# Scores of two heads on 64 rows each, 64-column state products in runs, and the state half's norm two chunks later, in a hybrid S5 and attention encoder layer

## The chip, the cores and the metric

One core of one Trainium2 chip runs the whole layer. The metric is the device time of one execution in microseconds (us). The engines are PE (TensorE, the matrix products), DVE (VectorE), ACT (ScalarE), POOL (GpSimd) and SP (SyncE, which issues most transfers).

## What is computed

One encoder layer on a sequence of 256 frames of width 2048, all in float32. Attention heads and a state space model (S5) share the input projection; their outputs are normed, joined, projected and added to the input; a convolved feed-forward part follows. Cut to what matters here:

```python
proj = x @ w_in                                  # q | k | v | u, 1024 columns each
scores = einsum(q, k) * 64 ** -0.5 + bias        # 16 heads of 64, chunk-causal band
attn = softmax(scores) @ v
s = scan(exp(dt * a), u @ B);  ssm = Re(C s) + D * u     # 64 groups, 64 states, 16 channels
ssm = gelu(ssm);  ssm = ssm * sigmoid(ssm @ w_glu + b_glu)
x = LayerNorm(alpha * x + concat(rmsnorm(attn), rmsnorm(ssm)) @ w_out)
hidden = gelu(causal_dwconv3(x @ W_gate)) * (x @ W_val)
out = LayerNorm(alpha * x + hidden @ w_ffn_out)
```

## The kernel before

**Main products.** Every weight matrix is streamed in chunks of 128x1024 floats. The loop `run` takes them in a fixed order; for chunk j it issues the load of chunk j+7 on SP (L148), and has chunk j+3 split into a high part `hi` (ACT, L163) and the rest `lo` (DVE, L164). Four buffers hold each of `raw`, `hi` and `lo`, so a split waits until PE has used the chunk four before. A chunk of the k and q projections (`kq`, chunks 32 to 63, four to each pair of heads: two of k, two of q) is 16 products on PE (L209 with 512 columns, L211 with 256), one of the v projection (chunks 24 to 31 near this change) is 12 (L245, L247, L249). These are called mains below.

**Side products.** The state space model and the attention of each pair of heads run as generators beside that loop. Small products go into a queue through `put(f, cost)`. After each main, `fill()` adds one credit (at most two are kept) and issues queued products until their costs have used it up, so a cost of 0.25 lets four products through for one main, and a cost of 0 lets all through at once. A scheduler then orders each engine's instructions by its own model, so the order on an engine is not that of the code alone.

**The parts that the change touches.** `ll` (L778) gives the local states: 4 groups x 2 parts (real, imaginary), named ll00 to ll31, each of 16 products that fill 64 of the 128 columns of the array (`tile_position=(0, 64 * g2)`), at cost 0.25; `drained()` makes a generator wait until the queue is empty. `ks` (L873) gives the kernel of the first block in 64 products at cost 0.5. When all `ll` are done (`loc_done`), POOL clears the tile `Kt` (L900), which takes the place of `loc`, SP fills it by eight small transfers (L907), and DVE runs the scan over chunks of the sequence (L844 to L847, 21 steps of four instructions). `CM` (L943, L944, L948) are the output matrices of the state space model, computed on DVE, the last of them `CM3`. `y` (L973) multiplies `Kt`, `X` and `CM`. For each pair of heads j, `evac_k` adds the two halves of the k product into `kz[0]` and `kz[1]` (L501, 64 partitions each; the other 64 partitions of each were cleared at the start), `evac_q` writes `qt` (L506), `scores(h)` gives S of head h in two products over all 128 rows (L1048, L1049), DVE adds the bias and finds the maximum (L1061), ACT takes the exponential, PE transposes (T, L1071) and multiplies by v (O, L1084). `kz` and `qt` have one buffer each, so the next pair's are written after this pair's S.

**The norm of the state half.** `evac_os(0)` first calls `rms(1)`: two products with a column of ones on PE (L1028) over `sqs`, to which POOL adds a square for each of eight blocks (L1012), a root on ACT, a reciprocal on DVE; then DVE scales and adds (L1168) and takes statistics (L1174). It stands after chunk (nb, c) = (1, 0) of the output projection of the state half (`os`). The chunks of that stage are 12 mains each; chunks of later column blocks are split into tiles that are kept (`held`).

Of the kernel before, what the change touches and what calls it, by code (L numbers as in the profile page):

```python
# [118 lines left out]
class Builder:  # L119
# [15 lines left out]
    def put(self, f, cost=1.0):  # L135
        self.queue.append((f, cost))
# [155 lines left out]
    def plan_phase1(self):  # L292
# [117 lines left out]
        for nb in range(4):  # L410
            for c in range(4):
# [26 lines left out]
                if nb == 0:  # L438
                    post = None
                elif (nb, c) == (1, 0):  # L440
                    post = lambda: self.evac_os(0, cur["po", 0], (0, 1))
                elif c < 3:
                    post = None
                self.add(I["wo"][8 * nb + 4 + c], mm, post, hold)

        self.kz = [ap.tile([P, SEQ], F32, name=f"kz{h}") for h in range(2)]
        self.qt = ap.tile([P, SEQ], F32, name="qt")
# [48 lines left out]
    def evac_k(self, j, ps):  # L496
        nc = self.nc
        t = self.evac_ab(ps, f"kb{j}")
        for h in range(2):
            r = slice(64 * h, 64 * h + 64)  # L500
            nc.vector.tensor_tensor(self.kz[h][r], ps[r, 0:SEQ], t[r], op=ALU.add)  # L501

# [6 lines left out]
    def s5_load(self):  # L509
# [9 lines left out]
        nc.gpsimd.memset(loc[64:128, :, :, :, 0:64], 0.0)  # L519
        nc.gpsimd.memset(self.kz[0][64:128], 0.0)  # L520
        nc.gpsimd.memset(self.kz[1][0:64], 0.0)

# [229 lines left out]
    def s5_loc(self):  # L752
# [20 lines left out]
        def ll(q, ri):  # L773
# [11 lines left out]
            for i in range(8):  # L785
                for g2 in range(2):
                    put(lambda i=i, g2=g2: mm(i, g2), 0.25)
            put(evac, 0)

        def both(f, pg):  # L790
            for ri in range(2):
                f(pg, ri)
# [26 lines left out]
        yield  # L819
        both(ll, 2)  # L820
        both(ll, 3)
        yield from drained()
# [39 lines left out]
    def s5_kstack(self):  # L862
# [14 lines left out]
        for i in range(16):  # L877
            for ri in range(2):
                for h in range(2):
                    self.put(lambda i=i, ri=ri, h=h: mm(i, ri, h), 0.5)  # L880
        while self.queue:
# [154 lines left out]
    def attention(self, j):  # L1036
        nc, ap, I = self.nc, self.ap_, self.I
        kz, qt = self.kz, self.qt
        v = self.res1
# [5 lines left out]

        def scores(h):
            ps = st["S", h] = self.bank(5 + h, f"S{j}{h}")
            nc.tensor.matmul(ps[:, 0:256], lhsT=qt[:, P:2 * P], rhs=kz[h], start=True, stop=True)  # L1048
            nc.tensor.matmul(ps[:, 256:384], lhsT=qt[:, 0:P], rhs=kz[h][:, 0:P], start=True, stop=True)  # L1049

# [62 lines left out]
        load(1)  # L1113
        scores(0)
        scores(1)
        yield
# [272 lines left out]
```

## Time and profile before

| what | value |
|---|---|
| median of 3 runs | 1141.27 us (1140.03 to 1142.17) |
| the profiled execution's own time | 1141.15 us |
| span of its profile | 1139.3 us |
| PE busy | 1110.3 us, 97% |
| DVE busy | 774.4 us, 68% |
| ACT busy | 566.6 us, 50% |
| mean granted clock of PE | 0.991 |

Times in rows count from the start of the span. An instruction's row gives its start, its duration, engine, line and operation, the tiles (out<-in), sizes, a count, and in brackets how long the engine stood idle before it and what ended that. A float32 product shows as two rows on PE (x2), and durations of neighbours overlap, so the cost of a product on PE is read from start to start. A granted clock of 1.00 is 2.4 GHz, 0.50 is 1.2 GHz.

### The profile page before, as it was taken

The numbers are of one execution on the slowest core, as the hardware profiler recorded it, in microseconds if no ns is written. First come the engines' busy times: TensorE is split into PE (matmuls) and PEld (weight loads), VectorE is DVE, ScalarE is ACT, GpSimd is POOL, SyncE is SP. The second block draws the span as 40 slices with busy tenths as digits, with TensorE's granted clock in tenths as the row PEclk, the third lists the DMA queues.
The fourth block names the chain that finished last, engine by engine and source line by source line (L and its number), as shares of the span: only waits on it lengthen the run. The fifth ranks groups of instructions, "written<-read, shape, count | busy, mean of one in ns | idle before, by whom it ended". The sixth has DMA issues, their size and how long they took to land.

```text
span 1139.3 us, 17905 instructions
## 1 busy us (share of the span) xinstructions
PE 1110.3 (97%) x6980; PEld 948.8 (83%) x6980; DVE 774.4 (68%) x1230; ACT 566.6 (50%) x882; POOL 75.5 (7%) x75
## 2 busy tenths in 40 slices
PE   8999979999999999999999999999999999999996
PEld 6887768888887888888888888888888888888885
DVE  7996889946588776666666666666666575454555
ACT  5455325537575565555555555555555443433350
POOL 2021300000011000000000000000000550000002
PEclk9999979999999999999999999999999999999998
DMA  8886334534766366666666666666666876666661
GB/s 303 279 226 164 118 122 139 162 96 138 244 188 201 108 204 186 185 188 185 188 188 188 186 187 186 186 185 185 189 186 187 307 223 197 190 198 190 192 195 74
DMA packets 61572, 212.03 MB, mean 186 GB/s; under 512 B 7344, under 2 KB 10800, under 8 KB 60592
## 3 DMA queue, kind: packets, MB, share of 16 engines
q1 hardware_dynamic: 59728, 204.18, 58.9%
q0 software_dynamic: 1472, 6.29, 1.8%
q8 instruction: 54, 0.88, 0.3%
q10 hardware_dynamic: 288, 0.43, 0.1%
q14 instruction: 30, 0.25, 0.1%
HBM read 207.46 MB, written 3.41 MB: 185 GB/s over the span
## 4 chain that ended last, share of the span: by engine, by line
PE 93%; DVE 4%; ACT 1%; issue 1%; DMA 1%; SPq 0%; POOL 0%; ACTq 0%; POOLq 0%
PE f L231 29%; PE f L224 15%; PE d L245 7%; PE d L249 7%; PE d L247 7%; PE kq L209 5%; PE u L209 2%; PE kq L211 2%; PE oa L249 1%; PE oa L245 1%; PE oa L247 1%; PE u L211 1%; PE glu L209 1%; DVE lo L164 1%; PE os L249 1%; PE os L245 1%
## 5 line engine op out<-in xcount | busy, mean ns | idle before, releaser
L164 DVE TENSOR_TENSOR lo<-raw,hi 128x1024 fp32r<-128x1024 f32 (+1 forms) x358 | 446.3, 1249 | 210.6 <-ACT hi L163 207.0
L163 ACT CAST hi<-raw 128x1024 fp32r<-128x1024 f32 (+1 forms) x358 | 374.3, 1047 | 300.0 <-PE d L249 116.9
L231 PE MATMUL f<-x1s,hi 128*128 128x512 f32 (+1 forms) x1408 | 487.2, 396 | 1.5 <-DVE x1s L1211 1.5
L224 PE MATMUL f<-x1s,lo 128*128 128x256 f32 x1408 | 380.0, 281 | 0.0
L231 PEld LDWEIGHTS f<-x1s,hi 128*128 128x128 f32 x1408 | 258.8, 188 | 57.6 <-DVE x1s L1211 1.8
L224 PEld LDWEIGHTS f<-x1s,lo 128*128 128x128 f32 x1408 | 265.8, 189 | 8.6
L247 PE MATMUL d<-lo,hid 128*128 128x512 f32 (+1 forms) x360 | 133.4, 371 | 0.0
L245 PE MATMUL d<-hi,hid 128*128 128x512 f32 (+1 forms) x360 | 133.4, 370 | 0.0
L249 PE MATMUL d<-hi,hid 128*128 128x512 f32 (+1 forms) x360 | 133.3, 370 | 0.0
L209 PE MATMUL kq<-xs,hi 128*128 128x512 f32 x240 | 92.8, 422 | 5.1 <-DVE qt L506 2.6
L247 PEld LDWEIGHTS d<-lo,hid 128*128 128x128 f32 x360 | 67.9, 188 | 11.7
L249 PEld LDWEIGHTS d<-hi,hid 128*128 128x128 f32 x360 | 67.8, 188 | 11.7
L245 PEld LDWEIGHTS d<-hi,hid 128*128 128x128 f32 x360 | 67.9, 188 | 11.5
L211 PE MATMUL kq<-xs,lo 128*128 128x256 f32 x240 | 69.8, 291 | 0.0
L209 PEld LDWEIGHTS kq<-xs,hi 128*128 128x128 f32 x240 | 47.0, 196 | 15.8 <-DVE qt L506 2.7
L1319 ACT COPY ga<-f 128x256 f32<-128x256 f32 x44 | 16.4, 372 | 83.3 <-PE f L231 83.3
L1326 DVE TENSOR_TENSOR gp<-f,ga 128x256 f32<-128x256 f32 x44 | 18.8, 426 | 45.6 <-ACT ga L1319 45.6
L1319 ACT COPY va<-f 128x256 f32<-128x256 f32 x44 | 16.4, 372 | 66.1 <-PE f L231 66.1
L1338 DVE TENSOR_TENSOR va<-f,va 128x256 f32<-128x256 f32 x44 | 18.7, 425 | 43.0 <-ACT va L1319 43.0
L211 PEld LDWEIGHTS kq<-xs,lo 128*128 128x128 f32 x240 | 47.2, 197 | 0.8
L209 PE MATMUL u<-xs,hi 128*128 128x512 f32 x120 | 43.5, 401 | 0.0
L1305 POOL DMA_DIRECT2D gb<-rows x4 | 2.2, 554 | 531.6 <-PE f L231 531.6
(228 smaller groups left out, 1366.9 us busy)
## 6 DMA issues: line engine op xcount, KB each, us to landing
raw<-wf SPq DMA_DIRECT2D x176, 512.0 KB, 3.7
raw<-wd SPq DMA_DIRECT2D x88, 512.0 KB, 4.1
raw<-wkq SPq DMA_DIRECT2D x32, 512.0 KB, 3.7
raw<-wo SPq DMA_DIRECT2D x32, 512.0 KB, 4.0
raw<-wu SPq DMA_DIRECT2D x16, 512.0 KB, 4.7
raw<-wv SPq DMA_DIRECT2D x15, 512.0 KB, 6.2
raw<-wg SPq DMA_DIRECT2D x8, 512.0 KB, 3.7
gb<-rows POOLq DMA_DIRECT2D x4, 1024.0 KB, 13.1
```

The source lines that it names most:

```text
L163: self.nc.scalar.copy(hi[:, c], raw[:, c])
L164: self.nc.vector.tensor_tensor(lo[:, c], raw[:, c], hi[:, c].bitcast(F32), op=ALU.subtract)
L209: nc.tensor.matmul(ps, start=first and kk == 0, stop=False, **h)
L211: nc.tensor.matmul(ps[:, 0:SEQ], start=False, stop=False, **l)
L224: nc.tensor.matmul(th(ps), lhsT=lo[:, w], rhs=th(x), start=False, stop=False)
L231: nc.tensor.matmul(ps[:, c], lhsT=hi[:, w], rhs=x[:, c], start=start and part is None, stop=stop)
L245: nc.tensor.matmul(ps, lhsT=ah, rhs=wh, start=first and kk == 0, stop=False)
L247: nc.tensor.matmul(ps, lhsT=ah, rhs=wl, start=False, stop=False)
L249: nc.tensor.matmul(ps, lhsT=al, rhs=wh, start=False, stop=last and kk == 1)
L1319: self.nc.scalar.copy(tv, v[:, :, 1])
L1326: nc.vector.tensor_tensor(g[:, 2:].rearrange("p (t c) -> p t c", t=2), p0, t, op=ALU.add)
L1338: nc.vector.tensor_tensor(tv, p0, tv, op=ALU.add)
```

## The change

The two adds of `evac_k` become one add into one tile `kt` of 128 partitions; the memsets of `kz` go. `scores` issues four products for both heads, each over 64 rows of the array (rows 0 to 63 for head 0, 64 to 127 for head 1), 256 columns for both heads first, then 128 for both. The cost of the `ll` and `ks` products becomes 0, and a `drained()` stands between ll2 and ll3. `evac_os(0)` moves from after chunk (1, 0) to after chunk (1, 2).

```diff
--- before.py
+++ after.py
@@ -437,13 +437,13 @@
                     hold = lambda m=4 * nb + c - 8: self.hold1(m)
                 if nb == 0:
                     post = None
-                elif (nb, c) == (1, 0):
+                elif (nb, c) == (1, 2):
                     post = lambda: self.evac_os(0, cur["po", 0], (0, 1))
                 elif c < 3:
                     post = None
                 self.add(I["wo"][8 * nb + 4 + c], mm, post, hold)
 
-        self.kz = [ap.tile([P, SEQ], F32, name=f"kz{h}") for h in range(2)]
+        self.kt = ap.tile([P, SEQ], F32, name="kt")
         self.qt = ap.tile([P, SEQ], F32, name="qt")
         self.sqs = ap.tile([P, SEQ], F32, name="sqs")
         self.cm_ready = self.mb_ready = 0
@@ -496,9 +496,7 @@
     def evac_k(self, j, ps):
         nc = self.nc
         t = self.evac_ab(ps, f"kb{j}")
-        for h in range(2):
-            r = slice(64 * h, 64 * h + 64)
-            nc.vector.tensor_tensor(self.kz[h][r], ps[r, 0:SEQ], t[r], op=ALU.add)
+        nc.vector.tensor_tensor(self.kt, ps[:, 0:SEQ], t, op=ALU.add)
 
     def evac_q(self, j, ps):
         nc = self.nc
@@ -517,8 +515,6 @@
         loc = self.loc = bp.tile([P, 2, 2, 8, P], F32, tag="d1", name="loc")
         nc.gpsimd.memset(loc[0:64, :, :, :, 64:128], 0.0)
         nc.gpsimd.memset(loc[64:128, :, :, :, 0:64], 0.0)
-        nc.gpsimd.memset(self.kz[0][64:128], 0.0)
-        nc.gpsimd.memset(self.kz[1][0:64], 0.0)
 
     def s5_late_load(self):
         nc, I = self.nc, self.I
@@ -784,7 +780,7 @@
                 nc.scalar.copy(self.L8[:, ri, q * 8:q * 8 + 8], v[:, :, 56:64])
             for i in range(8):
                 for g2 in range(2):
-                    put(lambda i=i, g2=g2: mm(i, g2), 0.25)
+                    put(lambda i=i, g2=g2: mm(i, g2), 0)
             put(evac, 0)
 
         def both(f, pg):
@@ -818,6 +814,7 @@
             yield
         yield
         both(ll, 2)
+        yield from drained()
         both(ll, 3)
         yield from drained()
         self.loc_done = True
@@ -877,7 +874,7 @@
         for i in range(16):
             for ri in range(2):
                 for h in range(2):
-                    self.put(lambda i=i, ri=ri, h=h: mm(i, ri, h), 0.5)
+                    self.put(lambda i=i, ri=ri, h=h: mm(i, ri, h), 0)
         while self.queue:
             yield
         ps = st[0]
@@ -1035,7 +1032,7 @@
 
     def attention(self, j):
         nc, ap, I = self.nc, self.ap_, self.I
-        kz, qt = self.kz, self.qt
+        kt, qt = self.kt, self.qt
         v = self.res1
         st = {}
 
@@ -1043,10 +1040,15 @@
             b = st["b", h] = ap.tile([P, 256], F32, tag="band", bufs=2, name=f"bd{j}{h}")
             nc.sync.dma_start(b, I["band"][2 * j + h])
 
-        def scores(h):
-            ps = st["S", h] = self.bank(5 + h, f"S{j}{h}")
-            nc.tensor.matmul(ps[:, 0:256], lhsT=qt[:, P:2 * P], rhs=kz[h], start=True, stop=True)
-            nc.tensor.matmul(ps[:, 256:384], lhsT=qt[:, 0:P], rhs=kz[h][:, 0:P], start=True, stop=True)
+        def scores():
+
+            for h in range(2):
+                st["S", h] = self.bank(5 + h, f"S{j}{h}")
+            for t in range(2):
+                for h in range(2):
+                    r = slice(64 * h, 64 * h + 64)
+                    o, q, n = ((st["S", h][:, 0:256], slice(P, 2 * P), 256), (st["S", h][:, 256:384], slice(0, P), 128))[t]
+                    nc.tensor.matmul(o, lhsT=qt[r, q], rhs=kt[r, 0:n], start=True, stop=True, tile_position=(64 * h, 0))
 
         def soft(h):
 
@@ -1111,8 +1113,7 @@
 
         load(0)
         load(1)
-        scores(0)
-        scores(1)
+        scores()
         yield
         soft(0)
         yield
```

The cost 0 also changes what the scheduler puts where. On PE, before, ll1 was interleaved with the mains of chunk 30 (`v12` and `v15` are v's sums, `hi30` and `lo30` the chunk's parts):

```order
L245 MATMUL v12_920<-hi30_1066,xs_78 128x512
L778 MATMUL ll10_1203<-up_638,loc_90 64x64 x5
L247 MATMUL v12_920<-lo30_1067,xs_78 128x512
L778 MATMUL ll10_1203<-up_638,loc_90 64x64 x4
L249 MATMUL v12_920<-hi30_1066,xs_78 128x512
L778 MATMUL ll10_1203<-up_638,loc_90 64x64 x4
L245 MATMUL v15_921<-hi30_1066,xs_78 128x512
L778 MATMUL ll10_1203<-up_638,loc_90 64x64 x3
L778 MATMUL ll11_1225<-up_638,loc_90 64x64
L247 MATMUL v15_921<-lo30_1067,xs_78 128x512
```

Now it is in one run after the first main of chunk 27 (`lt` are transposes that prepare ll):

```order
L247 MATMUL v15_918<-lo26_869,xs_78 128x512
L249 MATMUL v15_918<-hi26_868,xs_78 128x512
L245 MATMUL v12_917<-hi27_911,xs_78 128x512
L774 MATMUL ll10_1132<-up_635,loc_89 64x64 x16
L774 MATMUL ll11_1151<-up_635,loc_89 64x64 x16
L758 MATMUL lt30_1170<-ident_69,MB_176 128x128 x2
L247 MATMUL v12_917<-lo27_912,xs_78 128x512
```

All 32 products of ll1 moved together and three chunks earlier. ll2, which was in groups of about four between mains too, now has 21 products in a run and 11 single ones, each between two mains of chunk 36; ll3 is one run of 32 after chunk 37.

On PE at the first pair's scores, before (chunks 36 and 37 of k of the second pair):

```order
L209 MATMUL kq10_1492<-xs_78,hi36_1316 128x512
L211 MATMUL kq10_1492<-xs_78,lo36_1317 128x256
L1048 MATMUL S00_1532<-kz0_83,qt_85 128x256
L1049 MATMUL S00_1532<-kz0_83,qt_85 128x128
L1048 MATMUL S01_1535<-kz1_84,qt_85 128x256
L1049 MATMUL S01_1535<-kz1_84,qt_85 128x128
L209 MATMUL kq10_1492<-xs_78,hi37_1346 128x512
L211 MATMUL kq10_1492<-xs_78,lo37_1347 128x256
```

and now (chunk 35 is the last of q of the first pair, chunk 38 the first of q of the second; chunks 36 and 37 are done by then):

```order
L206 MATMUL kq02_1436<-xs_78,lo35_1333 128x256
L207 MATMUL kq02_1436<-xs_78,hi35_1332 128x512
L970 MATMUL y0_2367<-up_635,Kt_1424 32x64 x4
L970 MATMUL y1_2506<-up_635,Kt_1424 32x64
L1051 MATMUL S00_1532<-kt_83,qt_84 128x256
L1051 MATMUL S01_1533<-kt_83,qt_84 128x256
L1051 MATMUL S00_1532<-kt_83,qt_84 128x128
L1051 MATMUL S01_1533<-kt_83,qt_84 128x128
L209 MATMUL kq12_1580<-xs_78,hi38_1468 128x512
```

The scores stand directly behind the last chunk of their own q, and the first five products of `y` on `Kt` stand ahead of them; before, those products stood later, behind the scores, T and the first O.

On DVE, from the split of chunk 38 to `qt` of the first pair, before:

```order
L164 TENSOR_TENSOR lo38_1452<-raw38_1265,hi38_1451 128x1024
L844 TENSOR_TENSOR kcm_87<-X_869,QI_181 128x512
L845 TENSOR_TENSOR kcm_87<-X_869,kcm_87 128x512
L846 TENSOR_TENSOR kcm_87<-kcm_87,X_869 128x512
L506 SCALAR_TENSOR_TENSOR qt_85<-kq02_1352,qb0_1473 128x256
L847 TENSOR_TENSOR X_869<-kcm_87 128x64x8
```

where two more pieces of four such rows for CM3 (L943, L944, L948) stood between later steps of the scan. Now:

```order
L941 TENSOR_TENSOR kcm_86<-prm_79 128x512
L945 TENSOR_TENSOR CM3_1461<-kcm_86 64x32x16 x2
L940 TENSOR_TENSOR kcm_86<-prm_79 128x512
L941 TENSOR_TENSOR kcm_86<-prm_79 128x512
L945 TENSOR_TENSOR CM3_1461<-kcm_86 64x32x16 x2
L164 TENSOR_TENSOR lo40_1539<-raw40_1403,hi40_1538 128x1024
L841 TENSOR_TENSOR kcm_86<-X_866,QI_178 128x512
L842 TENSOR_TENSOR kcm_86<-X_866,kcm_86 128x512
L843 TENSOR_TENSOR kcm_86<-kcm_86,X_866 128x512
L164 TENSOR_TENSOR lo41_1575<-raw41_1434,hi41_1574 128x1024
L844 TENSOR_TENSOR X_866<-kcm_86 128x64x8
L504 SCALAR_TENSOR_TENSOR qt_84<-kq02_1436,qb0_1490 128x256
```

All of CM3 stands ahead of the scan's first step, and `qt` has the splits of chunks 40 and 41 and a whole step of the scan (L841 to L844 now) ahead of it. At the norm of the state half, 19 mains that stood behind the two products of `rms` now stand ahead of them, and on DVE three splits stand ahead of its reciprocal.

## Rows read from the trace of the kernel before

**Rows 1.** What PE waited for, over the whole span: the waiting line, the releaser, us in total, times, the longest.

```profile
PE kq L209 <- DVE qt L506: 2.6, 1, 2.6
PE kq L209 <- DVE kz L501: 2.5, 2, 2.1
PE T L1071 <- ACT sT L1065: 2.4, 2, 2.0
```

**Rows 2.** Stretches of the span: from:to, its length, then busy us (and instructions) of PE, PEld, DVE, ACT and POOL, the granted clock of PE, the share and rate of the DMA engines. The first rows are whole stages, the last four are 2 us each.

```profile
131.00:145.00 14.00, 14.00 (x82) 12.25 (x81) 13.52 (x26) 5.68 (x11) 3.39 (x1) 1.00 0.60 168
145.00:177.00 32.00, 23.61 (x125) 19.27 (x124) 27.50 (x61) 11.32 (x31) 0.00 (x0) 0.79 0.36 112
177.00:222.00 45.00, 45.00 (x280) 40.11 (x279) 44.32 (x106) 25.89 (x67) 0.00 (x0) 1.00 0.52 157
...
400.00:1139.00 739.00, 728.45 (x3949) 627.52 (x3947) 458.41 (x561) 352.27 (x483) 38.00 (x24) 1.00 0.63 191
...
150.00:152.00 2.00, 0.00 (x0) 0.00 (x0) 2.00 (x5) 0.00 (x0) 0.00 (x0) 0.55 0.48 74
...
156.00:158.00 2.00, 2.00 (x10) 1.68 (x10) 2.00 (x7) 0.00 (x0) 0.00 (x0) 0.74 0.00 0
...
162.00:164.00 2.00, 0.55 (x3) 0.31 (x3) 1.88 (x3) 1.31 (x6) 0.00 (x0) 0.96 0.52 209
...
170.00:172.00 2.00, 2.00 (x11) 1.73 (x10) 0.32 (x1) 1.05 (x1) 0.00 (x0) 0.83 0.00 0
```

**Rows 3.** Mains of kq on PE: the first after a long wait and two more at half clock, the first after another long wait, then two that stand three pairs of mains apart at full clock.

```profile
152.36 0.80 PE L209 MATMUL kq<-xs,hi 128*128 128x512 f32 x1 [2.58 <-DVE qt L506]
...
153.17 0.63 PE L209 MATMUL kq<-xs,hi 128*128 128x512 f32 x1
...
153.81 0.63 PE L209 MATMUL kq<-xs,hi 128*128 128x512 f32 x1
...
165.66 0.79 PE L209 MATMUL kq<-xs,hi 128*128 128x512 f32 x1 [2.09 <-DVE kz L501]
...
176.91 0.40 PE L209 MATMUL kq<-xs,hi 128*128 128x512 f32 x1
...
177.97 0.40 PE L209 MATMUL kq<-xs,hi 128*128 128x512 f32 x1
```

**Rows 4.** ll on PE: the run of ll0 between two mains of v, then two mains 42 apart with nothing between them, then a group of four ll products (eight rows) between two mains.

```profile
84.47 0.48 PE L249 MATMUL v<-hi,xs 128*128 128x512 f32 x1
84.88 2.08 PE L778 MATMUL ll<-up,loc 128*64 128x64 f32 x64
...
86.98 0.48 PE L245 MATMUL v<-hi,xs 128*128 128x512 f32 x1
...
87.76 0.39 PE L245 MATMUL v<-hi,xs 128*128 128x512 f32 x1
...
97.29 0.39 PE L245 MATMUL v<-hi,xs 128*128 128x512 f32 x1
...
98.92 0.50 PE L249 MATMUL v<-hi,xs 128*128 128x512 f32 x1
99.35 0.45 PE L778 MATMUL ll<-up,loc 128*64 128x64 f32 x8
99.73 0.50 PE L245 MATMUL v<-hi,xs 128*128 128x512 f32 x1
```

**Rows 5.** The scores of one head (its two lines, two rows each) and the first main behind both heads' scores, on PE.

```profile
142.03 0.59 PE L1048 MATMUL S<-kz,qt 128*128 128x256 f32 x2
...
142.46 0.38 PE L1049 MATMUL S<-kz,qt 128*128 128x128 f32 x2
...
143.25 0.47 PE L209 MATMUL kq<-xs,hi 128*128 128x512 f32 x1
```

**Rows 6.** DVE from the last ll to the first scores, and the two adds into kz of a later pair.

```profile
130.75 1.23 DVE L164 TENSOR_TENSOR lo<-raw,hi 128x1024 fp32r<-128x1024 f32 x1 [3.49 <-ACT hi L163]
131.89 0.69 DVE L844 TENSOR_TENSOR kcm<-X,QI 128x512 f32<-128x512 f32 x1
...
134.18 0.42 DVE L506 SCALAR_TENSOR_TENSOR qt<-kq,qb 128x256 f32<-128x256 f32 x1 [0.40 <-ACT qb L469]
...
135.12 1.23 DVE L164 TENSOR_TENSOR lo<-raw,hi 128x1024 fp32r<-128x1024 f32 x1
136.26 0.69 DVE L943 TENSOR_TENSOR kcm<-prm 128x512 f32<-128x512 f32 x1
...
137.59 1.39 DVE L948 TENSOR_TENSOR CM<-kcm 64x512 f32<-64x512 f32 x2
139.00 1.23 DVE L164 TENSOR_TENSOR lo<-raw,hi 128x1024 fp32r<-128x1024 f32 x1
...
175.49 0.85 DVE L501 TENSOR_TENSOR kz<-kq,kb 64x256 f32<-64x256 f32 x2
```

**Rows 7.** Kt: the memset on POOL, the eight transfers on SP, and the time from issue to landing of those eight.

```profile
130.85 3.54 POOL L900 MEMSET Kt<- 128x4096 f32 x1 [11.61 <-ACT hi L163]
...
134.42 4.19 SPq L907 DMA_DIRECT2D Kt<-kdr  x8
...
DMA to landing us min/median/max: 1.7/2.4/3.8
```

**Rows 8.** The two products of the state half's norm on PE.

```profile
354.08 0.61 PE L1028 MATMUL rms<-ones,sqs 128*128 128x1 f32 x4 [1.25 <-POOL sqs L1012]
```

## The prediction

> **What bounds the kernel now.** I read the busy times first, in the table: PE is busy for 97% of the span and no other engine comes near, so a microsecond is won where PE does less or waits less. Then the list of what PE waited for, to find the waits that are large: the long ones lie on the k and q projections (`qt`, `kz`, T on `sT`) [rows 1]; one of 1.25 us at the norm stands alone [rows 8]. Then the stretches, to see where these lie: from 145 to 177 PE is busy for 23.61 of 32.00 us, so it waits 8.4 us there, while from 177 to 222 it never waits; from 400 to the end it is busy for 728.45 of 739 us [rows 2]. A lead that PE has at about 220 us is therefore kept to the end, apart from the norm's stage.
>
> The clock column of the same stretches shows a second loss. The mean clock falls to 0.55 in 150 to 152, is 0.74 in 156 to 158, 0.96 in 162 to 164 and 0.83 in 170 to 172 [rows 2]. With levels of 1 and 0.5 that makes half speed from 150.2 to 157.0 and from 163.8 to 170.7, 6.8 us each; the mean of 0.79 over 32 us, 13.4 us at half, agrees. PE had a wait of 2.6 us before the first and two of 2.0 and 2.1 us, close together, before the second [rows 1]; the short waits are followed by no such row. A pair of mains takes 153.81 - 153.17 = 0.64 us then and (177.97 - 176.91) / 3 = 0.353 us at full clock [rows 3], so 45% of PE's time at half speed is lost. PE ran again from 152.36 and from 165.66 [rows 3], 9.7 us of those stretches, which lost 4.4 us. The stage loses 8.4 + 4.4 = 12.8 us.
>
> Its cause is DVE, which is busy for 13.52 of 14, 27.50 of 32 and 44.32 of 45 us from 131 to 222 [rows 2]. `qt` and `kz` stand in one line with the splits, the scan and CM3, and come late.
>
> **The runs of ll.** A main of v takes (97.29 - 87.76) / 42 = 0.227 us. The run of ll0 puts its neighbours 86.98 - 84.47 = 2.51 us apart, so 32 products cost 2.51 - 0.23 = 2.28 us; its two neighbours on either side are slowed a little by transposes, and I take 2.2 us: 0.063 us a product and about 0.2 us for going in and out. A group of four costs 99.73 - 98.92 - 0.23 = 0.58 us: 0.25 us of products and 0.33 us for in and out [rows 4]. ll1 was 8 such groups, 4.7 us, and becomes a run of 2.2: -2.5 us. ll2 and ll3 were 16 groups, 9.3 us. Now: a run of 21 (1.5), 11 single products, and a run of 32 (2.2). No single product is in the trace; it costs between 0.06 us (as in a run) and 0.58 us (as a group of four), and I take 0.33 + 0.06 = 0.39, since a visit pays the change of shape whatever its length: 4.3 us. Sum 8.0, -1.3 us. The ks products were one run already and stay one: nothing. Together **-3.8 us**, between -7.4 and -1.7.
>
> **The scores.** A pair of heads costs 143.25 - 142.03 = 1.22 us, that is 2 x 0.43 and 2 x 0.2 about [rows 5]. Products on 64 rows are not in the trace. The nearest rows are ll, on half the columns: two of them side by side take 2 x 0.063 = 0.125 us, where one of 256 columns at 0.43 us makes 0.107 us for 64 columns, 0.21 for two [rows 4, 5]; so they run largely at once. If the two heads do so too, the four products take 0.65 us at best, 0.75 with ll's loss, and 0.2 to 0.33 us for in and out: 0.85 to 1.08 us, a gain of 0.14 to 0.37. If they do not, 1.22 + 0.33, a loss of 0.33. I take a gain of 0.28, as ll shows halves at once: 8 x 0.28 = **-2.2 us**, between -3.0 and +2.6.
>
> The trace shows that entering and leaving a half-column shape costs 0.2 to 0.33 us [rows 4]. The Trainium skill (TensorEngine Tiling (Array Packing), Key Properties) says that changing the tiling mode drains TensorE, while tiles run independently; that rule speaks against eight more visits, and by it alone, without overlap, the scores would lose the 2.6 us above. The skill's TensorE: Matmul & The Clock Gate (Part 3) gives the opposite weight: row tiles start some 4 ns apart and a pack lasts little longer than one product, which would put the estimate at the 0.65 us end. No run here shows either for row tiles.
>
> **One add for k.** A pair of adds takes 0.85 us [rows 6], one of 128 partitions about as long as `qt`'s single instruction, 134.52 - 134.18 = 0.34 us to the next: 0.43 to 0.5 us of DVE less for each of 8 pairs. It lies on PE's path only where DVE is late, so it counts in the stage below. The two memsets at the start on POOL hide nothing and cost nothing.
>
> **The stage from ll to the third pair's scores.** Let T be the end of the last ll. DVE's steps from start to start: a split 1.14 us (135.12 to 136.26), a whole step of the scan about 2.4 (0.6 each, 131.89 on), four CM rows 139.00 - 136.26 = 2.74 us [rows 6]. In the new order:
> - The split of 39 waits for the buffer that chunk 37 frees, 2.2 us before T, and ACT's cast of about 1 us, so it ends near T. Behind it come 7 rows of CM3 (4.6), the split of 40 (1.14), three scan rows (1.8), the split of 41 (1.14), one scan row (0.6) and `qt` (0.42): T + 9.7.
> - Kt: the memset takes 3.54 us [rows 7] and starts at T + 0.2. Eight transfers then take 4.19 us to issue; the first and the fifth are what y's products read, and land about 2.4 us after issue (1.7 to 3.8): T + 8.3, at the latest T + 9.7.
> - On SP the loads of chunks 40 to 43 stand ahead of those eight; the last waits for the split of 39, near T, so they are out before the memset ends.
> - PE does chunks 34 and 35 (16 x 0.177 each) by T + 5.7. Then y, at the head of its queue, waits for Kt, and S behind it for `qt`. y's five products are hidden in the wait for `qt`, apart from 0.3 us. PE waits **3.7 us** (2.5 to 5).
> - A clock drop came 0.4 us after the first long wait began (152.36 - 2.58 = 149.8), and in the other case 0.3 us into the second of two waits; both held 6.8 us [rows 2, 3]. Here, 0.4 to 2.8 us after T + 5.7, it would hold until T + 12.9 to T + 15.3, so 3.2 to 5.6 us of mains run at half speed: 1.4 to 2.5, I take **1.9 us**.
> - Behind that the line on DVE reaches the second pair's `qt` at T + 20.4 and the third's at T + 35.8; PE, by chunks of 2.83 us with S, T and O between, reaches those scores at T + 21.2 and T + 36.4. No wait, but with only 0.6 us to spare, and T and O hang on ACT: I allow **1.0 us** of small waits.
>
> That is 6.6 us in place of 12.8: **-6.2 us**. What made room is that CM3 (5.4 us) stands in time that DVE had idle: it waited 3.49 us just before 130.75 [rows 6].
>
> **The norm.** PE waits 1.25 us for POOL's last square. With 19 mains (19 x 0.227 = 4.3 us) ahead of it, the square is done: **-1.2 us**, between -1.3 and 0. On ACT the root and its table load come behind three casts; DVE's reciprocal and scaling behind three splits of about 1.2 us; the sums that they free are wanted by the next norm's transposes only, behind some 80 mains (18 us). If that cover were gone, 3.5 us would be lost.
>
> **Sum.** -3.8 - 2.2 - 6.2 - 1.2 = -13.4 us. The profiled execution took 1141.15 us, 0.1 below the median: about **1128 us**.
>
> **The rivals.**
> - *DVE becomes the bound.* For the stretch from T on, DVE was busy 13.5 + 27.5 + 44.3 = 85.3 us; less CM3 (5.4), two splits (2.3) and five pairs' adds (2.1), plus the 4.6 us of CM3 left over at T, that is 80 us. PE's need is 91 - 12.8 - 2.8 - 1.4 + 6.6 = 80.6 us: a tie [rows 2]. If DVE stands idle for ACT's casts as it did before (91 - 85.3 = 5.7 us), the waits come back in small pieces, and two of over 2 us would bring 2 us of half clock each: 5.1 + 4 us of the gain gone, **1137 us**. For it speaks the 0.6 us to spare, against it that the order follows the chunks regularly now.
> - *The scores do not overlap.* +2.6 in place of -2.2: **1133 us**.
> - *Kt and `qt` come early enough* (the wait under 2 us, no clock drop): 5 us more gained, **1123 us**. Kt's own 8.3 us against PE's 5.7 speaks against it.
> - *Slower: the array drains between any two score products.* The halves alternate, four products in each pair of heads. If each waited for the end of the one ahead, their row lengths add up, 0.59 + 0.59 + 0.38 + 0.38 = 1.94 us [rows 5], and five changes at 0.33 us make 3.6 us, 2.4 more than before, eight times: +19 in place of -2.2, **1149 us**. It decides from (13.4 - 2.2 + 2.3) / 8 = 1.7 us lost on each pair. Against it: ll alternates halves too, at 0.063 us a product.
>
> **How the numbers follow.** Forecast 0.54; DVE as the bound 0.20; no overlap 0.09; early Kt 0.09; slower 0.08. The range, 1121 to 1138, takes in all but the last and the tails of the bounds. A measurement of this kernel tells about 0.2%, 2.3 us, from no change. All cases but the slower one end below 1138.9; I leave 0.06 for a DVE-bound stage that eats the rest: faster 0.86, same 0.06, slower 0.08.
>
> **What would show it.** ll1 as one run of about 2.2 us, 11 singles of 0.3 to 0.5 us; a pair's scores in 0.85 to 1.1 us from the first to the next main (1.5 would say no overlap, 3 a drain); one wait of 3 to 5 us on PE some 6 us behind the last ll, on Kt or `qt`, with one half-clock stretch, and no other wait over 1 us up to 200 us; none on POOL at the norm. It is wrong if PE waits for `qt` or `kt` again and again between that place and 220 us, or if the last scan row on DVE comes behind the first y product that wants it.

## The result, and the profile after

| what | value |
|---|---|
| median after | 1130.08 us (1128.40, 1128.61, 1131.55 and 1132.08) |
| median before, same chip | 1141.42 us |
| ratio | 0.9907, 95% interval 0.9895 to 0.9918 |
| the profiled execution's own time | 1131.55 us |
| span of its profile | 1129.7 us |

The forecast was 1128.0 us, range 1121 to 1138. The change is faster by 0.93%, as forecast, and the time lies in the range. The four executions stand in two pairs 3 us apart; the profiled one is of the longer pair, and the forecast lies 0.5 us below the shorter.

The list of what PE waited for, over the whole span (waiting line, releaser, us, times, longest), answers to [rows 1]:

```profile
PE kq L209 <- issue: 2.3, 1, 2.3
PE y L970 <- DMA Kt<-kdr: 2.3, 1, 2.3
PE S L1051 <- DVE qt L504: 1.8, 1, 1.8
...
PE v L247 <- DVE lo L164: 0.5, 1, 0.5
PE y L970 <- DVE ysh L971: 0.3, 2, 0.2
```

The waits for k's add and for T are gone, and so is the one on POOL. In their place stand one on `Kt` and one on `qt`, which were forecast, and one on "issue", which was not. The same stretches as in [rows 2], with the columns of that group:

```profile
131.00:145.00 14.00, 9.98 (x57) 8.15 (x56) 13.80 (x24) 2.69 (x5) 3.03 (x1) 0.83 0.52 160
145.00:177.00 32.00, 32.00 (x197) 27.95 (x197) 30.96 (x88) 18.36 (x46) 0.00 (x0) 0.97 0.50 148
177.00:222.00 45.00, 42.67 (x435) 36.99 (x434) 40.85 (x91) 25.14 (x67) 0.00 (x0) 1.00 0.55 163
...
400.00:1129.00 729.00, 718.84 (x3892) 618.96 (x3890) 450.48 (x550) 345.22 (x472) 38.02 (x24) 1.00 0.62 190
140.00:142.00 2.00, 1.36 (x8) 1.19 (x8) 2.00 (x5) 0.00 (x0) 0.00 (x0) 0.55 0.89 311
...
146.00:148.00 2.00, 2.00 (x11) 1.76 (x10) 2.00 (x7) 0.63 (x1) 0.00 (x0) 0.74 0.22 66
```

PE is busy for all of 145 to 177, where it stood still for 8.4 us before; it loses 4.0 us between 131 and 145 instead. The clock says half speed from 140.2 (0.55 over two us) to 147.0 (0.74). A loss that was not there before lies in 177 to 222: PE is busy for 42.67 of 45 us. Its rows on PE, with those of ll and of a pair's scores (columns as in [rows 3] to [rows 5]):

```profile
89.42 0.39 PE L245 MATMUL v<-hi,xs 128*128 128x512 f32 x1
89.74 2.08 PE L774 MATMUL ll<-up,loc 128*64 128x64 f32 x64
91.75 0.44 PE L758 MATMUL lt<-ident,MB 128*128 128x128 f32 x2
...
115.51 0.40 PE L207 MATMUL kq<-xs,hi 128*128 128x512 f32 x1
115.84 1.50 PE L774 MATMUL ll<-up,loc 128*64 128x64 f32 x42
117.41 0.50 PE L209 MATMUL kq<-xs,hi 128*128 128x512 f32 x1
...
118.67 0.33 PE L774 MATMUL ll<-up,loc 128*64 128x64 f32 x2
118.92 0.51 PE L209 MATMUL kq<-xs,hi 128*128 128x512 f32 x1
119.36 0.33 PE L774 MATMUL ll<-up,loc 128*64 128x64 f32 x2
...
124.98 0.33 PE L774 MATMUL ll<-up,loc 128*64 128x64 f32 x2
...
127.94 0.39 PE L207 MATMUL kq<-xs,hi 128*128 128x512 f32 x1
128.26 2.09 PE L774 MATMUL ll<-up,loc 128*64 128x64 f32 x64
130.28 0.50 PE L209 MATMUL kq<-xs,hi 128*128 128x512 f32 x1
...
138.46 0.43 PE L970 MATMUL y<-up,Kt 128*32 128x64 f32 x10 [2.27 <-DMA Kt<-kdr]
140.64 1.65 PE L1051 MATMUL S<-kt,qt 64*128 64x256 f32 x8 [1.75 <-DVE qt L504]
...
153.27 0.92 PE L1051 MATMUL S<-kt,qt 64*128 64x256 f32 x8
154.13 0.50 PE L209 MATMUL kq<-xs,hi 128*128 128x512 f32 x1
...
218.74 0.43 PE L970 MATMUL y<-X,vtok 128*32 128x64 f32 x16
219.10 0.33 PE L1075 MATMUL T<-ident,sT 128*128 128x128 f32 x1
221.75 0.50 PE L209 MATMUL kq<-xs,hi 128*128 128x512 f32 x1 [2.33 <-issue]
```

T, the end of the last ll, is 130.28. The eleven single products of ll2 stand between 118.67 and 124.98, each between two mains. Behind `y` PE stands still from 219.4 to 221.75 with no semaphore to wait for.

### The profile page after: what moved, and what is told of

Its sections match the earlier page's. It is cut to its first block, busy times and chain, and to the rows that moved or that the text cites. A ratio compares the mean times of both kernels' runs of the same rounds, so it can differ in the third digit from the quotient of the medians.

```text
span 1129.7 us, 17895 instructions
## 1 busy us (share of the span) xinstructions
PE 1104.6 (98%) x6980; PEld 944.4 (84%) x6980; DVE 769.9 (68%) x1222; ACT 566.0 (50%) x882; POOL 74.0 (7%) x73
## 4 chain that ended last, share of the span: by engine, by line
PE 94%; DVE 3%; DMA 1%; issue 1%; ACT 1%; SPq 0%; ACTq 0%
PE f L231 29%; PE f L224 15%; PE d L247 7%; PE d L249 7%; PE d L245 7%; PE kq L209 5%; PE u L209 3%; PE kq L211 2%; PE oa L245 1%; PE oa L247 1%; PE oa L249 1%; PE u L211 1%; PE glu L209 1%; PE os L245 1%; PE os L249 1%; PE os L247 1%
## 5 line engine op out<-in xcount | busy, mean ns | idle before, releaser
L231 PE MATMUL f<-x1s,hi 128*128 128x512 f32 (+1 forms) x1408 | 487.2, 396 | 1.5 <-DVE x1s L1212 1.5
L231 PEld LDWEIGHTS f<-x1s,hi 128*128 128x128 f32 x1408 | 258.8, 188 | 57.6 <-DVE x1s L1212 1.8
```

The source lines that it names most:

```text
L231: nc.tensor.matmul(ps[:, c], lhsT=hi[:, w], rhs=x[:, c], start=start and part is None, stop=stop)
```

## The experiments

Times are compared as ratios to the kernel before on the same chip; 0.001 is 1.14 us. "The theory" at first was that of the prediction: DVE's line is full, and CM3 ahead of the scan makes the room.

**The norm back.** The changed kernel with the norm of the state half where it was.

```diff
-                elif (nb, c) == (1, 2):
+                elif (nb, c) == (1, 0):
```

> The changed kernel with the state half's norm back after chunk (1, 0); the rest as changed. Theory (the move is worth the wait for POOL's last square): that wait of about 1.2 us comes back at the norm and the time is 1.0 us above the changed kernel's 1130.1, so 1131 (1130 to 1132.5). Rival (the wait is only moved, DVE's late scaling costs as much): no wait on POOL of over 0.5 us, time within 0.5 us of the changed kernel's.

Measured: 1128.86 us (1128.31 to 1129.50), 0.9899 [0.9885, 0.9914]: not slower than the changed kernel. The wait of 1.2 us on POOL is back, but the "issue" wait is 0.5 us here, not 2.3. So that stall, which no theory had, weighs more than the norm, whose stage is 0.9 us longer here (48.55 us from the first product of `os` to the first of `f`, L231, behind it; 47.63 in the changed kernel).

**The scores alone.** The kernel before with the one tile `kt` and the four row-half products; costs, `drained()` and the norm as before.

```diff
-        scores(0)
-        scores(1)
+        scores()
```

> The kernel before with only the row halves for the scores and the one add for k. Theory (the scores gain some 0.3 us a pair, and the stage from 145 to 177 us keeps its waits since the order there hardly changes): 8 x 0.3 = 2.4 us less than before, 1139 (1137 to 1140), and waits of over 1.5 us of PE on DVE remain there. Rival 1 (the shorter line on DVE is what empties that stage): 1133 or less. Rival 2 (no overlap): 1142 or more.

Measured: 1131.29 us, 0.9919 [0.9905, 0.9934]. The time is that of the expectation's first rival: PE is busy for 29.71 of 32 us in 145 to 177, though CM3 still stands among the steps of the scan. Room from CM3 is thus not needed. What moved besides the shorter line is the order: the second pair's `qt` starts at 149.78, ahead of three rows of the scan that it stood behind at 151.89 before, and on PE chunk 40 (the third pair's k) moves ahead of the rest of 42 and of 43 (its q). Which of the two empties the stage, this run alone does not tell.

**The runs of ll alone.** The kernel before with only the costs at 0 and the `drained()`.

```diff
-                    put(lambda i=i, g2=g2: mm(i, g2), 0.25)
+                    put(lambda i=i, g2=g2: mm(i, g2), 0)
...
+        yield from drained()
...
-                    self.put(lambda i=i, ri=ri, h=h: mm(i, ri, h), 0.5)
+                    self.put(lambda i=i, ri=ri, h=h: mm(i, ri, h), 0)
```

> The kernel before with only the costs of ll and ks at 0 and the stop between ll2 and ll3; here ll2 and ll3 come in runs without single products. Theory (the runs are worth 3.8 us and 1 to 3 more without singles, and the new order of the stage behind ll another 6): 1129 to 1132, so most of the whole change's gain. Rival (the stage is emptied by the kt add and the shorter scores): 1136 to 1138.

Measured: 1128.04 us, 0.9892 [0.9877, 0.9906], at the low end of the theory's case, with waits of 2.4 us on `Kt`, 2.3 on `qt`, 1.8 on issue and 1.2 at the norm. The two parts alone gain 9.2 and 12.3 us and both together 10.6: each of them, by another order on DVE and PE, already takes a good part of the stage's loss of 12.8 us, which can be taken once. By the prediction's way of counting 3.8 us of it are left with the scores alone, 7.0 with the runs alone and 6.9 in the changed kernel.

**q first.** The changed kernel with the sums of the first pair's q put ahead on DVE. The first `y` products then come seven chunks later.

```diff
-        t = self.evac_ab(ps, f"qb{j}", 0.125)
-        nc.vector.scalar_tensor_tensor(self.qt, ps[:, 0:SEQ], 0.125, t, op0=ALU.mult, op1=ALU.add)
+        with self.tc.high_priority(300) if j == 0 else nullcontext():
+            t = self.evac_ab(ps, f"qb{j}", 0.125)
+            nc.vector.scalar_tensor_tensor(self.qt, ps[:, 0:SEQ], 0.125, t, op0=ALU.mult, op1=ALU.add)
```

> The changed kernel with the first pair's q evacuated at high priority, so that its add stands ahead of the scan's step on DVE and the scores stand ahead of y's first products. Theory (in the changed kernel the line on DVE ahead of qt, and Kt, cost PE 4.0 us of waits and 2.9 us of half clock): no wait of over 1.5 us there, no half clock, and 5 to 6 us less than the changed kernel, 1124 (1123 to 1126). Rival (DVE is full, so the wait comes back at the second or third pair): 1128 to 1131, with waits on qt or kt behind it.

Measured: 1123.66 us (1123.55 to 1123.70), 0.9853 [0.9837, 0.9870], a hit. Of the stage's waits one of 1.5 us on `qt` is left, at full clock (1.00 in 131 to 177).

**The same edit on the kernel before.**

> The kernel before with one edit: the q sums and add of the first pair ahead of the scan's steps on DVE; the order on PE is that of the kernel before, and scores, k, ll, costs and the norm are untouched. Theory (the first long wait hangs on the place of qt in DVE's line, not on DVE being full): the wait of 2.6 us at about 150 us and the half clock behind it (about 2.1 us lost) go, the waits on k's add and on T stay: 1140.1 - 4.5 = 1135.6 us (1134 to 1138). Rival (DVE has no time left in this stage, what qt gains the scan and the splits lose): 1139 to 1142 us, with the same microseconds of waiting elsewhere before 180 us.

Measured: 1140.68 us, 0.9999 [0.9990, 1.0008]. The expectation had the wrong `qt`: the first pair's stands at 134.18 already before [rows 6] and did not move (134.10), since it waits there for ACT's copy. The wait of 2.6 us is for the second pair's, at 151.89. The run tells nothing on the theories but that.

**q and k first, for all pairs, on the kernel before.** That edit without `if j == 0`, and the same around the sums of `evac_k`. Chunks 38 and 39 stand ahead of half of 36 on PE in the kernel before already, which the expectation has wrong; what the edit moves on PE comes later: chunks 40 and 41 (the third pair's k) now stand ahead of most of 42 and of 43 (its q).

> The kernel before with the sums and adds of q and of k of every pair ahead of what else stands on DVE; scores over full rows, ll in groups and the norm as before. The scheduler then puts chunks 38 and 39 ahead of half of 36 on PE. Theory (all of the stage's loss of 12.8 us hangs on q's and k's adds standing behind scan steps and CM3): most of it comes back, 10 us, 1130 us (1128 to 1133), with PE busy for over 30 of 32 us in 145 to 177 us at a clock of 0.95 or more. Rival (DVE is full from 131 to 222 us, the loss only changes place): 1138 to 1142 us, with waits on lo, X or CM in place of those on q and k.

Measured: 1129.97 us, 0.9906 [0.9892, 0.9919]: 11 us from the order alone, on DVE and PE, as much as the whole change. DVE around the second pair's `qt` in the kernel before (first fence) and in this one (second), columns as in [rows 6]:

```profile
147.52 1.39 DVE L948 TENSOR_TENSOR CM<-kcm 64x512 f32<-64x512 f32 x2
148.94 1.23 DVE L164 TENSOR_TENSOR lo<-raw,hi 128x1024 fp32r<-128x1024 f32 x1
150.08 0.68 DVE L844 TENSOR_TENSOR kcm<-X,QI 128x512 f32<-128x512 f32 x1
...
151.89 0.42 DVE L506 SCALAR_TENSOR_TENSOR qt<-kq,qb 128x256 f32<-128x256 f32 x1
```

```profile
148.10 0.42 DVE L508 SCALAR_TENSOR_TENSOR qt<-kq,qb 128x256 f32<-128x256 f32 x1
148.44 0.86 DVE L502 TENSOR_TENSOR kz<-kq,kb 64x256 f32<-64x256 f32 x2
149.34 1.39 DVE L950 TENSOR_TENSOR CM<-kcm 64x512 f32<-64x512 f32 x2
```

The same work stands there, `qt` 3.8 us earlier, ahead of CM, a split and three rows of a step of the scan. The stretch from 145 to 177 of this kernel:

```profile
145.00:177.00 32.00, 31.86 (x211) 28.15 (x210) 31.40 (x70) 16.16 (x39) 0.00 (x0) 1.00 0.45 134
```

PE is busy throughout at full clock, and DVE does 31.40 us of work where it did 27.50 [rows 2]. It had not been full. In the kernel before it idled for 4.5 of the 32 us, 2.9 of them in front of these two rows, waiting for scores from a PE that waited for it:

```profile
155.97 0.42 DVE L1061 CUSTOM_DVE_ANT_0 sT<-S,bd 128x256 f32<-128x256 f32 x1 [0.94 <-PE S L1049]
...
171.68 0.42 DVE L1061 CUSTOM_DVE_ANT_0 sT<-S,bd 128x256 f32<-128x256 f32 x1 [1.95 <-PE S L1049]
```

Up to the first long wait (2.6 us on `qt`) the order on PE is the same in both kernels, so that wait hung on DVE's order. For the later ones, on T and on k's add, DVE's order and the moved chunks on PE are not told apart.

**All of ll2 and ll3 in one run.** q first, and the products of ll given out early.

```diff
+                with self.tc.high_priority(100):
+                    nc.tensor.matmul(st[1][r, 64 * i:64 * i + 64], ...
```

> The changed kernel with two edits of order: the first pair's q sums and add ahead of the scan's steps on DVE (as in qt_first), and the products of ll given out early, so that ll2 and ll3 are one run of 64 ahead of chunk 36 and no single product is left; chunks 36, 37, 34 and 35 then lie between the last ll and the first y product. Theory (a single product between two mains costs about 0.45 us, one in a run 0.065): against qt_first, 1123.7 us, 11 x 0.39 = 4.3 us less, and the 11 us of chunks cover the clearing and filling of Kt (8 us): 1119.4 us (1118 to 1121), no wait on Kt, at most one wait over 1 us in 130 to 180 us. Rival (the singles cost no more than their share of a run, or DVE gives the time back as waits for its splits): 1123 to 1126 us, with new waits of mains on lo or hi.

Measured: 1121.29 us, 0.9824 [0.9811, 0.9838], 3.3 us less than q first by the ratios; 4.3 were expected. The 64 products take 4.1 us beside a main (115.76 to 120.12); in q first eight were single and three together, so 3.8 us were to be had. No wait on `Kt`, one of 1.7 us on `qt`.

**The score products in another order.** q first, with head 0's two products ahead of head 1's.

```diff
-            for t in range(2):
-                for h in range(2):
+            for h in range(2):
+                for t in range(2):
```

> qt_first (1123.7 us) with nothing changed but the order of the four score products of each pair of heads: head 0 with 256 and 128 columns, then head 1 with 256 and 128, in place of alternating row halves. Theory (products on different row halves run at once when they stand side by side): alternating, a pair is 0.43 + 0.22 + 0.21 = 0.86 us as measured; in the new order only head 0's 128 columns lie beside head 1's 256, 0.43 + 0.43 + 0.22 + 0.21 = 1.29 us. Eight pairs: +3.4 us, 1127.1 us (1126 to 1128), and about 1.3 us from the first S to the next main. Rival (the gain over full rows comes from something else, the row halves do not run at once): 1123.7 us (1123 to 1124.3), 0.86 us still.

Measured: 0.9850 [0.9835, 0.9865], 1124.4 us, and 0.86 us a pair: the theory of this expectation lost, the order makes no difference. Its rival had no overlap at all; the next run judges that.

**Both heads on one row half.** The same with rows 0 to 63 for all four products, so that head 1's scores are not computed.

```diff
-                    r = slice(64 * h, 64 * h + 64)
+                    r = slice(0, 64)
...
-                    ... tile_position=(64 * h, 0))
+                    ... tile_position=(0, 0))
```

> qt_first_serial_scores (1124.4 us) with all four score products of a pair on rows 0 to 63, so that head 1's scores are those of head 0 (part of the computation is left out); shapes and counts are the same. Theory (two row halves share TensorE's time; on one half the products' row lengths add up): 2 x 0.43 + 2 x 0.22 + 0.21 = 1.5 us for a pair in place of 0.86, eight pairs +5 us: 1129.5 us (1128 to 1131). Rival (a product on 64 rows is by itself shorter than one on 128, with no overlap of halves): 0.86 us a pair still, 1124.4 us (1123.5 to 1125).

Measured: 1127.95 us, 0.9885 [0.9871, 0.9898], 4.0 us more. The scores of a pair, between their neighbours on PE:

```profile
136.82 1.57 PE L1052 MATMUL S<-kt,qt 64*128 64x256 f32 x8 [1.50 <-DVE qt L505]
138.32 0.50 PE L209 MATMUL kq<-xs,hi 128*128 128x512 f32 x1
```

That is 1.50 us a pair in place of 0.86, as the theory had it, 8 x 0.64 = 5.1 us; the other waits of this run are 1 us less (the one on issue 0.7 us, in the other 1.3). So a product on 64 rows is not cheaper by itself: the gain comes from two halves at work at once.

**The products of `y` spread out.** The changed kernel with a chunk of mains between the two halves of each group of `y`.

```diff
                 nc.vector.tensor_copy(ysh[:, 2 * pg + f]...
+                if f == 0:
+                    yield
```

> The changed kernel with one edit: the products of y wait for a whole chunk of mains between the two halves of a group, so that runs of 44 to 48 short products stand a chunk apart in place of two runs with three to six products between them. Theory (PE's idle 2.3 us at 219 us, at which no wait of the program stands, comes from issuing two runs of short products close behind one another, and its executions of 1132 us against 1128.5 are those with that stall and half clock): no issue wait over 1 us and no half clock in 205 to 245 us, 1127.8 us (1126.5 to 1129) in all executions. Rival (the stall does not hang on the runs of y; or y's later end makes the state half's products wait for gathl): the stall is still there, or waits on gathl of over 1 us, 1129 to 1133 us.

Measured: 1125.16 us (1124.68 to 1125.81), 0.9859 [0.9846, 0.9873], by the ratios 5.5 us below the changed kernel, more than forecast. No wait on issue is left, and the four executions lie within 1.2 us. The windows from 177 to 250:

```profile
177.00:222.00 45.00, 45.00 (x452) 39.21 (x452) 40.77 (x91) 25.31 (x62) 0.00 (x0) 1.00 0.52 159
222.00:250.00 28.00, 28.00 (x598) 24.03 (x597) 12.87 (x29) 12.28 (x30) 0.00 (x0) 1.00 0.38 108
```

PE is never idle there, at full clock. The stage's waits are unchanged (2.2 on `Kt`, 1.8 on `qt`). What is gained beyond the stall and its half clock (4.0 us) are the small waits of `y` on issue and on `ysh`, DVE's copies of its sums (0.5 us), and, in the profiled execution, some half clock of the stage, which lasted 3.4 us there and 6.8 in the changed kernel's (1.5 us). These make 6.0 of the 6.9 us between the two profiled executions; where the rest lies is open.

**All of it, and the norm once more.** The run of 64 with `y` spread out, and that with the norm back after chunk (1, 0).

> qt_first_ll_whole (1121.3 us) with the same edit on y. Theory as in after_y_split: its issue wait of 0.8 us goes, 1120.3 us (1119.3 to 1121). Rival: no change or waits on gathl, 1121 to 1124 us.

> ll_whole_y_split with the norm of the state half back after chunk (1, 0), where the kernel before had it. Theory (PE waits for POOL's last square there and nothing else changes): a wait of 1.2 us on POOL is back, 1.2 us more than ll_whole_y_split (0.8 to 1.6). Rival (what the wait costs is given back at a later wait of the same stage): within 0.3 us of ll_whole_y_split.

Measured: 1118.24 us, 0.9797 [0.9784, 0.9810], and 1118.01 us, 0.9795 [0.9782, 0.9808]. The first gained 3 us, more than the 1 expected. It is the kernel that beats both, by 23 us against the kernel before and, by the ratios, 12.6 against the changed one. The norm's place makes no difference, but the wait on POOL did not come back either, so this does not measure the term; the last section has more on that wait.

A kernel with a buffer of its own for `Kt`, which would free its clearing from the last ll, was not tried.

## Why the prediction was right, and where it was not

- **The runs of ll**, forecast -3.8 us. ll1 took 91.75 - 89.42 - 0.23 = 2.1 us (forecast 2.2), the run of 21 1.7 (1.5), ll3 2.1 (2.2). The singles were mis-sized: from 118.67 to 124.98 ten products and ten mains take 6.31 us, 0.63 less a main's 0.18, so 0.45 us each in place of 0.39. The term measures -2.6 - 0.6 = **-3.2 us**.
- **The scores**, forecast -2.2. From the first S to the next main 154.13 - 153.27 = 0.86 us, before 1.22 [rows 5]: 8 x 0.36 = **-2.9 us**. The mechanism, halves at once, is shown by the run on one half. Both rivals on the array are out: no overlap would be 1.5 us a pair, a drain between products over 3. The Trainium skill (TensorEngine Tiling (Array Packing), Key Properties) says that a change of mode drains TensorE; that fits the 0.2 us a visit beside 0.43 + 0.22 of rows, and none is paid between the two halves. The Trainium skill (TensorE: Matmul & The Clock Gate, Part 3) says that a pack of row tiles lasts little longer than one product; that agrees, with 0.65 us for the four.
- **The stage**, forecast -6.2. Against T = 130.28: PE at `y` after 5.9 us (forecast 5.7), `Kt` after 8.2 (8.3), S after 10.4 (`qt` after 9.7). The waits were 2.27 + 1.75 = 4.0 us (forecast 3.7), the small ones nil (1.0). The half clock held from T + 9.9 to T + 16.7, as long as before but 1.4 to 3.8 us later than forecast, so more mains ran in it: 0.45 x (147.04 - 140.64) = 2.9 us (forecast 1.9, bound 2.5). Together 6.9 us in place of 12.8: **-5.9 us**.
- **The norm**, forecast -1.2. The wait on POOL is gone, and from the first product of `os` to the first of `f` the kernel before takes 48.56 us, the changed one 47.63: **-0.9 us**. The mains ahead of it do cover the square: in five kernels with the moved norm it takes 1.84 us, as before, and PE does not wait (47.5 to 47.9 us). In this profiled execution the cover was not put to the test, since the square took 0.74 us, at which PE waited at most 0.2 us at the old place too (last section).
- **The step that failed** is a clause behind the stage's sum, "What made room is that CM3 (5.4 us) stands in time that DVE had idle", and with it the rival in which DVE is the bound, at 0.20. CM3 did not go into that time. On DVE around T, in the changed kernel:

```profile
125.60 1.23 DVE L164 TENSOR_TENSOR lo<-raw,hi 128x1024 fp32r<-128x1024 f32 x1 [3.28 <-ACT hi L163]
...
130.59 0.69 DVE L941 TENSOR_TENSOR kcm<-prm 128x512 f32<-128x512 f32 x1
...
134.06 1.39 DVE L945 TENSOR_TENSOR CM<-kcm 64x512 f32<-64x512 f32 x2
```

The idle time is still there, 3.28 us where it was 3.49 [rows 6], and 4.9 us of CM3, from 130.59 to 135.45, still stand behind T; the prediction's own list has 4.6 there. Nor was room needed: with q and k first the stage's loss goes while CM3 stays among the scan, and the scores alone do nearly the same. What cost the 12.8 us was an order in which the adds that free PE stood behind work nobody waited for yet; how much of the later waits hung on PE's own order of chunks is open. "Its cause is DVE" was right of the line's order, wrong of its load. The size came out because the order, read row by row, gave the right moments, whatever made the room: the second and the third pair's `qt` started at T + 20.4 and T + 36.2 (forecast 20.4 and 35.8).
- **Not foreseen**: the stall of 2.33 us at 219.4 (the last section says what PE lacked) and half clock after it (0.50 in 223 to 225), some 1.7 us lost: **+4.0 us**. The prediction took a lead at 220 us as kept to the end and had no term for 215 to 230.

The sum by these is -3.2 - 2.9 - 5.9 - 0.9 + 4.0 = -8.9 us; the profiled executions differ by 1131.55 - 1141.15 = -9.6. The rest is about what small waits shrank by: `ks` waited 0.5 us for `vtok` and `y` 0.8 for `ysh` before, now nothing and 0.3. Without the stall the terms make -12.9, where -13.4 was forecast. The shorter pair of executions, -12.7 against the same, would be those without it. That is argued only: one of the four was profiled, q first and the norm back, whose runs of `y` stand as close, have one group each, and with `y` spread out the time lies another 3 us below the shorter pair.

## What to carry to other kernels

When PE waits for an engine that looks full, first read which row on that engine frees PE, and what stands ahead of it that nobody waits for yet: here an order with q's and k's adds earlier, by 3.8 us at the first long wait, gave as much as the whole change, and the engine then did more work in the same stretch. Parts that each reorder such a line are not to be added up. Runs of small products are cheaper than single ones (0.065 against 0.45 us here), but two long runs close behind one another can leave PE waiting for its next instructions, which a chunk of large products between them avoided here.

## What the runs showed of the hardware

**Row halves run at once, whatever their order in the queue.** With head 0's two products ahead of head 1's, the rows of one pair that lie in 165.70 to 165.90 and in 165.70 to 166.20 (count, shortest, median and longest in ns, first and last start):

```profile
L1052 PE MATMUL S<-kt,qt x2: 480/480/480, 165.8 to 165.8; 64*128 64x256 f32 x2
```

```profile
L1052 PE MATMUL S<-kt,qt x4: 376/428/480, 165.8 to 166.1; 64*128 64x256 f32 x4
```

Two rows of 256 columns begin at 165.8. A product shows as two rows, and with all four on one half these begin 0.3 us apart, so that a window of the same kind, 166.90 to 167.20 of that run, has one row:

```profile
L1052 PE MATMUL S<-kt,qt x1: 480/480/480, 167.0 to 167.0; 64*128 64x256 f32 x1
```

So one of the two rows at 165.8 is head 1's, which started ahead of head 0's 128 columns. The scheduler had kept the order of the code: in the program both products of S00 stand ahead of both of S01. In the trace the first two rows of a pair start 13 to 14 ns apart in this order and 6 to 7 ns in the alternating one. The Trainium skill (TensorE: Matmul & The Clock Gate, Part 3) says that products start and end strictly in the order of the program; these rows speak against it for products on different row halves, and the 0.86 us a pair, which by the rows' own lengths that order would make about 1.3 (an estimate, 0.43 + 0.43 + 0.22 + 0.21), decides for the rows.

**POOL's square and DVE's split shut one another out.** The last square ahead of the norm and the split beside it, on POOL and DVE, in the changed kernel:

```profile
343.49 0.74 POOL L1009 TENSOR_TENSOR sqs<-sqs,sq 128x256 f32<-128x256 f32 x1 [3.60 <-ACT sq L1008]
```

```profile
343.52 1.79 DVE L164 TENSOR_TENSOR lo<-raw,hi 128x1024 fp32r<-128x1024 f32 x1
```

and in the one with the norm back:

```profile
340.05 1.84 POOL L1009 TENSOR_TENSOR sqs<-sqs,sq 128x256 f32<-128x256 f32 x1 [3.59 <-ACT sq L1008]
```

```profile
340.08 1.22 DVE L164 TENSOR_TENSOR lo<-raw,hi 128x1024 fp32r<-128x1024 f32 x1
```

They start 0.03 us apart both times, and one of them takes 0.6 to 1.1 us more. In all fourteen profiled executions the square starts 0.02 to 0.03 us ahead of the split; it takes 0.74 us in four of them and 1.82 to 1.84 in ten, that of the kernel before among the ten. So the starts do not tell which of the two loses. With the norm at its old place PE waits 1.2 to 1.3 us in the five kernels where the square loses, and 0.2 us or nothing in the two where it wins, one of which is the last run of the study. The norm's wait of [rows 8] thus hangs on which of two nearly simultaneous instructions goes first. The Trainium skill (SBUF — State Buffer, Who interferes with whom) says that a DVE instruction with two inputs in SBUF and a GpSimd one that reads SBUF hold a shared port in turn, the later one blocked for the whole of the other; the first pair of rows fits that, 0.74 us of square and then 1.08 of split.

**PE can stand still with no wait in the program**, after some ninety products on 32 columns, because its next instructions are not there. The wait on issue was 0.4 to 2.5 us in sum in the kernels whose two runs of `y` stand close together, at varying places, and absent in the three with a chunk of mains between them. The DMA records tell what PE lacked. The queue named q8 brings blocks of 16384 bytes (first line: the whole of the changed kernel, with blocks, MB and the share of 16 engines); one comes for some 259 rows of PE and its weight loads, so it brings PE's instructions. One of its blocks starts when the stall of the changed kernel does (second line: 219.43 to 219.45):

```profile
q8 instruction: 54, 0.88, 0.3%
```

```profile
q8 instruction: 1, 0.02, 301.9%
```

It lands at 220.41, and PE goes on at 221.75, 2.3 us after the block's start. In each of the nine kernels with a wait on issue of 0.5 us or more that wait (the longest, where there are two) ends 2.3 to 2.5 us after the start of a block on q8 and 1.3 to 1.5 us after its landing. Why the block is asked for no earlier is open.
